# A batched 64x64 matmul on one core: a new order for GpSimd's list, for the casts and turns of VectorE, and for two loads of b

## The chip, the cores and the metric

The kernel runs on one core of a Trainium2 chip. The metric is device time in microseconds (us) from launch to end. A time is compared with runs of the kernel before on the same chip. "PE" is TensorE, "DVE" is VectorE, "ACT" is ScalarE, "POOL" is GpSimd and "SP" is SyncE, as the profile names them.

## The reference

```python
def setup_inputs():
    return {"a": np.random.randn(1024, 64, 64).astype(np.float32),
            "b": np.random.randn(1024, 64, 64).astype(np.float32)}

def reference(a, b):
    return np.matmul(a, b).astype(np.float32)
```

There are 1024 independent products of 64x64 matrices. Each of a, b and the output is 16.78 MB in float32, so 50.33 MB cross between HBM and the core.

## The kernel before

The batch is cut into 16 tiles (t) of 64 matrices, and two tiles make a pair (s = t // 2, eight pairs). A tile is multiplied as block-diagonal matmuls: a's matrices, transposed, stand as small blocks in a 128-row weight tile `at_bd`, and b's matrices stream through. There are two such weight tiles, `bd_tiles[t % 2]`, cleared once.

The steps of a pair s, with their lines:

- `load_a` (L81): three quarters of a's pair are cast to bf16 by GpSimd's DMAs (L76, three per pair), and the last quarter comes as float32 over SyncE (L88). `load_pair` (L112) brings both tiles of b by four casting DMAs on GpSimd's queue (L115). It does so for pairs 1 to 6. The b tiles 0, 1, 14 and 15 come singly as float32 through `load_b` (L104, one DMA of 1 MB, L109). The pools hold three buffers for a and three for b.
- `regroup` (L126): DVE puts the two parts of a side by side in `a_bf` (L130, L133).
- `transpose` (L137): 16 PE transposes per pair into PSUM (L142), 8 for each of j = 0 and j = 1, and four ACT copies to `at_sb` (L145).
- `spread` (L168): four DVE copies per tile put `at_sb` into the diagonal blocks of `at_bd` (L186; for pairs 0 and 1 eight smaller ones, L176). All four copies of one tile read what all four ACT copies of L145 wrote.
- `turn` (L118): a DVE transpose in 32x32 blocks for each half u of b's pair (L124). Every tile of the pair reads both halves.
- `cast` (L191): for b tiles 0, 1, 14 and 15 a copy to bf16 takes the place of the turns.
- `multiply` (L216): 64 matmuls (L247), in two halves of 32, each half into one of two PSUM buffers `o_ps`. `evacuate` (L229) copies each half to `o_sb` by four copies on L235. All of them are on ACT; from tile 10 on DVE takes two of the four copies of the second half, and in the last tile DVE takes half of all.
- `store` (L212): one DMA of 1 MB per tile (L224) on GpSimd's queue, made one tile later than the multiply (`HOLD = 2`). Tile 14 is stored in two pieces and tile 15 in four, on ACT and SyncE.

`tc.manual_schedule()` means that each engine runs its instructions exactly in the order in which the code below L268 writes them; a wait holds everything that is queued behind it on that engine. So the order of the calls in the loop over t is the order on PE, ACT, DVE, and on the queues of GpSimd and SyncE. `multiply(t)` contains its evacuation, so ACT copies of a later call follow the copies of tile t.

Before, the loop works ahead by about two pairs: `spread(t + 1)` stands in front of `multiply(t)`; `regroup(s + 2)` and the first half of `transpose(s + 2)` are made while pair s is multiplied, the second half of the transposes one tile before they are needed, and the turns of the next pair one after each tile. GpSimd's list has the loads of pairs 1 to 4 of b and a up to pair 4 ahead of the first store.

Of the kernel before, what the change touches and what calls it, by code (L numbers as in the profile page):

```python
# [13 lines left out]
def kernel(  # L14
# [14 lines left out]
    nc = tc.nc  # L29
# [8 lines left out]
    HOLD = 2  # L38
    PAIRS = (1, 2, 3, 4, 5, 6)
    ON_DVE = (0, 1)  # L40
    FIRST_B = {1: nc.scalar}

    a_v = a.rearrange("(s g h) (mp v) k -> s h g mp (v k)", h=4, g=32, v=16)
    bp_v = b.rearrange("(s g h) k n -> s h g (k n)", h=4, g=32)
# [36 lines left out]
    def load_a(s, a_sb=None):  # L81
        a_sb = a_sb or cast_load_a(s)
        a_raw = a_pool.tile([128, 16, 64], fp32, name="a_raw")[:].rearrange("p v k -> p (v k)")
        if s in ON_DVE:
            a_raw = a_raw.bitcast(bf16)[:, 0:1024]
            nc.gpsimd.dma_start(out=a_raw, in_=a_v[s, 3], single_packet=True)
        else:
            nc.sync.dma_start(out=a_raw, in_=a_v[s, 3])  # L88
        a_tiles[s] = a_sb, a_raw
# [14 lines left out]
    def load_b(t):  # L104
        b_sb = b_pool.tile([128, 1, 4096], bf16, name="b_sb")[:, 0].bitcast(fp32).rearrange(
            "p (g c) -> p g c", g=16
        )
        queue = FIRST_B.get(t, nc.sync)
        queue.dma_start(out=b_sb, in_=b_v[t])  # L109
        b_tiles[t] = b_sb  # L110

    def load_pair(s):  # L112
        pair = b_pool.tile([128, 1, 4096], bf16, name="b_sb")
        for h in range(4):
            nc.gpsimd.dma_start(out=pair[32 * h : 32 * h + 32, 0], in_=bp_v[s, h])  # L115
        b_tiles[2 * s] = pair
# [20 lines left out]
    def transpose(s, j):  # L137
        a_cols = abf_tiles[s][:].rearrange("p v h k -> p v (h k)").bitcast(fp32)
        for wl in range(2):
            at_ps = t_psum.tile([128, 4, 128], fp32, name="at_ps")  # L140
            for vo in range(4):
                nc.tensor.transpose(  # L142
                    at_ps[:, vo, :], a_cols[:, 4 * vo + 2 * j + wl, :], identity[:]
                )
            nc.scalar.copy(  # L145
                at_tiles[s][:, :, 2 * j + wl, :, :],
                at_ps[:].rearrange("p vo (g mp) -> p g mp vo", mp=4),
            )
# [19 lines left out]
    def spread(t, hs=range(4), copy=nc.vector.tensor_copy):  # L168
        bd = bd_tiles[t % N_BD]
        at_sb = at_tiles[t // 2]  # L170
        for h in hs:
            rows = slice(32 * h, 32 * h + 32)
            if t // 2 in ON_DVE:
                for i in range(2):
                    block = 32 * (2 * (t % 2) + i)
                    copy(  # L176
                        bd[rows, 8 * i : 8 * i + 8, :, h, :, :].rearrange(
                            "p g w mp vo -> p (g w) (mp vo)"
                        ),
                        at_sb[block : block + 32, h].rearrange(  # L180
                            "p g w mp vo -> p (g w) (mp vo)"
                        ),
                    )
            else:
                half = slice(16 * (t % 2), 16 * (t % 2) + 16)
                nc.vector.tensor_copy(  # L186
                    bd[rows, :, :, h, :, :].rearrange("p g w mp vo -> p (g w) (mp vo)"),
                    at_sb[rows, half].rearrange("p g w mp vo -> p (g w) (mp vo)"),
                )
# [26 lines left out]
    def multiply(t):  # L216
        at_bd = bd_tiles[t % N_BD][:].rearrange("p g (j wl) h mp vo -> p j g (wl h mp vo)", j=2)
        at_bd = at_bd.bitcast(bf16).rearrange("p j g (c u) -> p j g c u", u=2)
        b_bf = bbf_tiles[t // 2][:, 16 * (t % 2) : 16 * (t % 2) + 16]
        last = t == n_t - 1  # L220
        o_sb = o_pool.tile([128, 8, 2, 2, 64], fp32, name="o_sb")

        def put(lo, n):
            store_queue(t, lo).dma_start(  # L224
                out=o_v[t, :, lo : lo + n, :],
                in_=o_sb[:, lo : lo + n].rearrange("p gh j wl n -> p (gh j wl n)"),
            )

        def evacuate(o_ps, gh, n, copies):  # L229

            for par in range(2):
                for wl in range(2):
                    src = o_ps[64 * wl : 64 * wl + 64, :, par, :, :]
                    dst = o_sb[64 * par : 64 * par + 64, gh : gh + n, :, wl, :]
                    copies[2 * par + wl](dst, src)  # L235

        for half in range(2):
            if not last:
                o_ps = o_psum.tile([128, 4, 2, 2, 64], fp32, name="o_ps")
            for g8 in range(8):  # L240
                if last and g8 % 4 == 0:
                    o_ps = t_psum.tile([128, 2, 2, 2, 64], fp32, name="at_ps")
                g = 8 * half + g8
                gl = (g8 % 4 if last else g8) // 2
                for j in range(2):
                    for u in range(2):
                        nc.tensor.matmul(  # L247
                            o_ps[:, gl, g % 2, j, :],
                            at_bd[:, j, g, :, u],
                            b_bf[:, g, 64 * u : 64 * u + 64],  # L250
                            start=(u == 0),
                            stop=(u == 1),
                        )
                if last and g8 % 4 == 3:
                    copy = nc.scalar.copy if g8 == 3 else nc.vector.tensor_copy
                    evacuate(o_ps, g // 4 * 2, 2, [copy] * 4)
            if not last:
                copies = [nc.scalar.copy] * 4
                if half and t > 9:
                    copies[2:] = [nc.vector.tensor_copy] * 2  # L260
                evacuate(o_ps, 4 * half, 4, copies)
        if last:
            held[t] = [lambda q=q: put(2 * q, 2) for q in range(4)]
        else:
            whole = t < n_t - 2
            held[t] = [lambda q=q: put(q, 8 if whole else 4) for q in ([0] if whole else [0, 4])]

    with tc.manual_schedule():  # L268
        load_first_a()
        nc.vector.memset(warm[:, 0:1], 0.0)  # L270
        nc.scalar.copy(warm[:, 1:2], warm[:, 0:1])
        load_b(0)
        load_b(1)
        nc.vector.memset(bd_tiles[0][:], 0.0)  # L274
        nc.gpsimd.memset(bd_tiles[1][:], 0.0)  # L275
        load_a(1)
        make_identity(nc, identity)
        load_pair(1)
        load_a(2)
        turn_a(0, 0)  # L280
        spread(0, [0])
        turn_a(0, 1)
        spread(0, [1])
        turn_a(0, 2)
        turn_a(0, 3)
        spread(0, [2], nc.scalar.copy)
        spread(0, [3])
        spread(1)
        cast(0)
        load_pair(2)  # L290
        load_a(3)
        for t in range(n_t):
            s, half = t // 2, t % 2
            if 0 < t < n_t - 1:
                spread(t + 1)
            if t + 1 < n_t:
                cast(t + 1)
            if t == 0:
                load_pair(3)
            if t in (8, 10):  # L300
                load_b(14 + (t - 8) // 2)
            if half == 0 and 1 < s < n_s - 1:
                transpose(s + 1, 1)
            multiply(t)
            if t == 0:
                for h in range(4):
                    turn_a(1, h)
                a_tiles.pop(1)
                load_a(4)
            elif t == 1:  # L310
                turn(1, 0)
                turn(1, 1)
                load_pair(4)
            elif t == 2:
                regroup(2)
                load_a(5)
                transpose(2, 0)
                transpose(2, 1)
                turn(2, 0)
                turn(2, 1)  # L320
                load_pair(5)
            elif t == 3:
                regroup(3)
                load_a(6)
                transpose(3, 0)
            else:
                if s + 1 in PAIRS:
                    turn(s + 1, half)
                    if half and s + 4 in PAIRS:
                        load_pair(s + 4)  # L330
                if half == 0 and s + 2 < n_s:
                    regroup(s + 2)
                    if s + 5 < n_s:
                        load_a(s + 5)
                elif half == 1 and s + 2 < n_s:
                    transpose(s + 2, 0)
            if t >= HOLD - 1:
                store(t - HOLD + 1)
        for t in range(n_t - HOLD + 1, n_t):
            store(t)  # L340

# [29 lines left out]
```

## Time and profile before

| what | value |
|---|---|
| time, median of 3 runs | 135.55 us (134.97 to 136.09) |
| time of the profiled execution | 135.04 us |
| its span, first to last instruction | 133.1 us |
| granted TensorE clock, mean | 0.822 |
| busy: DVE / ACT / PE / POOL | 107.1 / 89.1 / 61.1 / 49.0 us |
| HBM read / written | 33.55 MB / 16.78 MB, 378 GB/s over the span |

The span leaves out 1.94 us that the execution spends around it. Busy times are sums over the span, and their sizes alone do not tell which engine sets the end. In a row of the timeline, "[x <-Y]" means that the engine sat idle for x us before the row and that Y released it.

### The profile page before, as it was taken

How to read it: one execution, taken by the hardware profiler on the slowest of the kernel's cores; microseconds unless marked ns; L12 is line 12 of the kernel's file. 1: busy time of each engine (PE TensorE's matmuls, PEld its weight loads, DVE VectorE, ACT ScalarE, POOL GpSimd, SP SyncE). 2: the span in 40 equal slices, each digit the busy share in tenths (PEclk: the TensorE clock that was granted, in tenths of full speed). 3: DMA queues.
4: the chain of work that ended last, by engine and by line, in shares of the span. 5: the costliest groups of instructions: out<-in, count | busy, mean ns of one | idle time of the engine just before them, and what ended most of it. 6: DMA issues, size and time to landing. Idle time of an engine off the chain costs nothing.

```text
span 133.1 us, 2777 instructions
## 1 busy us (share of the span) xinstructions
PE 61.1 (46%) x1120; PEld 58.3 (44%) x1120; DVE 107.1 (81%) x135; ACT 89.1 (67%) x154; POOL 49.0 (37%) x69
## 2 busy tenths in 40 slices
PE   0000019646490098385763649853028377296000
PEld 0000018636490097385752549853027377285000
DVE  5999849899879994599999999964399948999900
ACT  2364049993999356999999999998206097659300
POOL 8981113432642624270765531345400403042200
PEclk9999999996899757997799985699955955559955
DMA  3999999999999999999999999999999999999992
GB/s 89 393 348 305 313 310 260 245 282 229 197 221 270 209 209 243 222 339 294 227 230 331 259 358 274 337 292 247 387 401 406 397 356 352 329 342 329 317 341 71
DMA packets 13068, 38.45 MB, mean 289 GB/s; under 512 B 1280, under 2 KB 2304, under 8 KB 12288
## 3 DMA queue, kind: packets, MB, share of 16 engines
q0 software_dynamic: 8416, 27.79, 78.2%
q1 hardware_dynamic: 3280, 7.87, 16.8%
q10 hardware_dynamic: 1360, 2.62, 5.3%
q8 instruction: 9, 0.15, 0.4%
q14 instruction: 3, 0.02, 0.1%
HBM read 33.55 MB, written 16.78 MB: 378 GB/s over the span
## 4 chain that ended last, share of the span: by engine, by line
DMA 47%; DVE 17%; ACT 14%; PE 9%; issue 4%; POOL 3%; DVEq 0%; POOLq 0%
DMA a_sb<-in_a_dram 37%; ACT o_sb L235 13%; DMA out_dram<-o_sb 10%; DVE at_bd L186 6%; PE o_ps L247 6%; DVE o_sb L235 5%; PE at_ps L142 3%; DVE b_bf L124 2%; ACT at_sb L145 2%; POOL at_bd L275 1%; DVE a_bf L130 1%; POOL a_sb L76 1%; DVE b_bf L203 1%; DVE a_bf L133 1%; DVE b_bf L208 1%
## 5 line engine op out<-in xcount | busy, mean ns | idle before, releaser
L235 ACT COPY o_sb<-o_ps 64x512 f32<-64x512 f32 x110 | 63.9, 581 | 11.6 <-PE o_ps L247 10.1
L247 PEld LDWEIGHTS <-at_bd 128*128 128x128 bf16 x1024 | 43.5, 113 | 49.5 <-issue 27.4
L247 PE MATMUL o_ps<-b_bf,at_bd 128*128 128x64 bf16 x960 | 43.7, 217 | 46.2 <-ACT b_bf L200 19.5
L186 DVE COPY at_bd<-at_sb 32x1024 f32<-32x1024 f32 x48 | 35.0, 728 | 1.2
L124 DVE STREAM_TRANSPOSE b_bf<-b_sb 128x1024 f32<-128x1024 f32 x12 | 26.4, 2218 | 5.9 <-DMA b_sb<-in_b_dram 5.7
L224 POOL DMA_DIRECT2D out_dram<-o_sb x16 | 16.5, 1032 | 37.4 <-issue 14.7
L142 PE MATMUL at_ps<-identity,a_bf 128*128 128x128 f32 x96 | 16.8, 349 | 14.2 <-DVE a_bf L133 14.2
L115 POOL DMA_DIRECT2D b_sb<-in_b_dram x24 | 14.9, 623 | 18.1 <-DMA b_sb<-in_b_dram 5.9
L142 PEld LDWEIGHTS at_ps<-identity,a_bf 128*128 128x128 f32 x96 | 15.1, 184 | 14.5 <-issue 8.2
L145 ACT COPY at_sb<-at_ps 128x512 f32<-128x512 f32 x24 | 12.9, 596 | 11.0 <-issue 6.2
L76 POOL DMA_DIRECT2D a_sb<-in_a_dram x21 | 13.0, 618 | 19.0 <-DMA a_sb<-in_a_dram 15.9
L176 DVE COPY at_bd<-at_sb 32x512 f32<-32x512 f32 x30 | 12.7, 423 | 0.7
L235 DVE COPY o_sb<-o_ps 64x512 f32<-64x512 f32 x10 | 6.9, 689 | 3.4 <-ACT o_sb L235 3.3
L130 DVE COPY a_bf<-a_sb 128x3072 bf16<-128x3072 bf16 x6 | 5.7, 947 | 3.8 <-DMA a_sb<-in_a_dram 3.8
L155 ACT CAST a_bf<-o_sb 128x1024 bf16<-128x1024 f32 x3 | 3.0, 1044 | 3.5 <-DMA o_sb<-in_a_dram 3.5
L200 ACT CAST b_bf<-b_sb 128x1024 bf16<-128x1024 f32 x1 | 1.0, 1044 | 6.2 <-DMA b_sb<-in_b_dram 6.2
L133 DVE CAST a_bf<-a_raw 128x1024 bf16<-128x1024 f32 x6 | 4.1, 690 | 0.0
L274 DVE MEMSET at_bd<- 128x4096 f32 x1 | 3.5, 3472 | 0.8 <-issue 0.8
L163 DVE STREAM_TRANSPOSE at_sb<-a_bf 128x512 f32<-128x512 f32 x4 | 4.0, 1041 | 0.1
L275 POOL MEMSET at_bd<- 128x4096 f32 x1 | 3.5, 3511 | 0.3 <-POOLq L355 0.3
L235 DVE COPY o_sb<-at_ps 64x256 f32<-64x256 f32 x8 | 3.4, 422 | 0.1
L235 ACT COPY o_sb<-at_ps 64x256 f32<-64x256 f32 x8 | 2.9, 366 | 0.1
(21 smaller groups left out, 17.3 us busy)
## 6 DMA issues: line engine op xcount, KB each, us to landing
out_dram<-o_sb POOLq DMA_DIRECT2D x14, 1024.0 KB, 15.0
b_sb<-in_b_dram POOLq DMA_DIRECT2D x24, 256.0 KB, 12.4
a_sb<-in_a_dram POOLq DMA_DIRECT2D x21, 256.0 KB, 11.8
a_raw<-in_a_dram SPq DMA_DIRECT2D x6, 512.0 KB, 11.9
o_sb<-in_a_dram SPq DMA_DIRECT2D x2, 512.0 KB, 5.4
o_sb<-in_a_dram ACTq DMA_DIRECT2D x2, 512.0 KB, 6.4
out_dram<-o_sb POOLq DMA_DIRECT2D x2, 512.0 KB, 6.9
out_dram<-o_sb ACTq DMA_DIRECT2D x2, 256.0 KB, 6.0
```

The costliest lines, as they stand in the source:

```text
L76: nc.gpsimd.dma_start(out=a_sb[:, h, :, :].rearrange("p v k -> p (v k)"), in_=a_v[s, h], single_packet=True)
L115: nc.gpsimd.dma_start(out=pair[32 * h : 32 * h + 32, 0], in_=bp_v[s, h])
L124: nc.vector.transpose(cols[:, u], rows[:, u])
L130: nc.vector.tensor_copy(a_bf[:, :, 0:3, :], cast_sb[:].rearrange("p h v k -> p v h k"))
L133: nc.vector.tensor_copy(a_bf[:, :, 3, :], raw.rearrange("p (v k) -> p v k", v=16))
L142: nc.tensor.transpose(at_ps[:, vo, :], a_cols[:, 4 * vo + 2 * j + wl, :], identity[:])
L145: nc.scalar.copy(at_tiles[s][:, :, 2 * j + wl, :, :], at_ps[:].rearrange("p vo (g mp) -> p g mp vo", mp=4),)
L176: copy(bd[rows, 8 * i : 8 * i + 8, :, h, :, :].rearrange("p g w mp vo -> p (g w) (mp vo)"), at_sb[block : block + 32, h].rearrange("p g w ...
L186: nc.vector.tensor_copy(bd[rows, :, :, h, :, :].rearrange("p g w mp vo -> p (g w) (mp vo)"), at_sb[rows, half].rearrange("p g w mp vo -> p ...
L224: store_queue(t, lo).dma_start(out=o_v[t, :, lo : lo + n, :], in_=o_sb[:, lo : lo + n].rearrange("p gh j wl n -> p (gh j wl n)"),)
L235: copies[2 * par + wl](dst, src)
L247: nc.tensor.matmul(o_ps[:, gl, g % 2, j, :], at_bd[:, j, g, :, u], b_bf[:, g, 64 * u : 64 * u + 64], start=(u == 0), stop=(u == 1),)
```

## The change

From tile 0 on, the loop calls `multiply(t)` first. `regroup` and both halves of `transpose` work on the next pair (s + 1) and stand behind the multiply of the even tile. Behind the multiply of the odd tile stand the spread of the next even tile, both turns of the next pair, and the spread of the next odd tile. Loads move behind the stores: for t = 2, 4, 6 and 8 GpSimd's list gets, after `store(t - 1)`, the load of b's pair s + 2 and of a's pair s + 3. The b tiles 14 and 15 are asked for by ACT in t = 10, in place of SyncE in t = 8 and 10. `cast(1)` stands ahead of the loop. DVE takes its two copies of the evacuation from tile 12 on, no longer from tile 10.

On GpSimd the list before goes, behind a's pair 3: b pair 3, a pair 4, b pair 4, store 0, a pair 5, b pair 5, store 1, a pair 6, store 2, a pair 7, store 3, b pair 6, stores 4 to 14. After it goes, behind a's pair 3: stores 0 and 1, b pair 3, a pair 4, stores 2 and 3, b pair 4, a pair 5, stores 4 and 5, b pair 5, a pair 6, stores 6 and 7, b pair 6, a pair 7, stores 8 to 14.

```diff
-    FIRST_B = {1: nc.scalar}
+    B_QUEUE = {0: nc.sync, 1: nc.scalar, 14: nc.scalar, 15: nc.scalar}
...
-        queue = FIRST_B.get(t, nc.sync)
-        queue.dma_start(out=b_sb, in_=b_v[t])
+        B_QUEUE[t].dma_start(out=b_sb, in_=b_v[t])
...
-                if half and t > 9:
+                if half and t > 11:
                     copies[2:] = [nc.vector.tensor_copy] * 2
...
         load_a(3)
+        cast(1)
         for t in range(n_t):
             s, half = t // 2, t % 2
-            if 0 < t < n_t - 1:
-                spread(t + 1)
-            if t + 1 < n_t:
-                cast(t + 1)
-            if t == 0:
-                load_pair(3)
-            if t in (8, 10):
-                load_b(14 + (t - 8) // 2)
-            if half == 0 and 1 < s < n_s - 1:
-                transpose(s + 1, 1)
             multiply(t)
             if t == 0:
                 for h in range(4):
                     turn_a(1, h)
                 a_tiles.pop(1)
-                load_a(4)
-            elif t == 1:
-                turn(1, 0)
-                turn(1, 1)
-                load_pair(4)
-            elif t == 2:
-                regroup(2)
-                load_a(5)
-                transpose(2, 0)
-                transpose(2, 1)
-                turn(2, 0)
-                turn(2, 1)
-                load_pair(5)
-            elif t == 3:
-                regroup(3)
-                load_a(6)
-                transpose(3, 0)
-            else:
-                if s + 1 in PAIRS:
-                    turn(s + 1, half)
-                    if half and s + 4 in PAIRS:
-                        load_pair(s + 4)
-                if half == 0 and s + 2 < n_s:
-                    regroup(s + 2)
-                    if s + 5 < n_s:
-                        load_a(s + 5)
-                elif half == 1 and s + 2 < n_s:
-                    transpose(s + 2, 0)
+            elif half == 0 and s + 1 < n_s:
+                regroup(s + 1)
+                transpose(s + 1, 0)
+                transpose(s + 1, 1)
+            elif half and s + 1 in PAIRS:
+                spread(t + 1)
+                turn(s + 1, 0)
+                turn(s + 1, 1)
+                spread(t + 2)
+            elif half and s + 1 < n_s:
+                for later in (t + 1, t + 2):
+                    spread(later)
+                    cast(later)
             if t >= HOLD - 1:
                 store(t - HOLD + 1)
+            if half == 0 and 0 < s < 5:
+                load_pair(s + 2)
+                load_a(s + 3)
+            if t == 10:
+                load_b(14)
+                load_b(15)
```

## The prediction

> **What bounds the kernel now.** I read the page's 40 slices first, then the timelines of ACT, DVE and PE.
>
> ```profile
> DMA  3999999999999999999999999999999999999992
> GB/s 89 393 348 305 313 310 260 245 282 229 197 221 270 209 209 243 222 339 294 227 230 331 259 358 274 337 292 247 387 401 406 397 356 352 329 342 329 317 341 71
> ```
>
> The DMA engines are never free between the first slice and the last. (GB/s counts a casting load by what it writes, half of what it reads, so the 200s of the middle are no slack.) 50.33 MB at the page's 378 GB/s are the whole 133.1 us: the kernel is bound by transfers, and the stores that wait fill the queue while the engines compute ahead. The compute rows show how far ahead. ACT, then DVE:
>
> ```profile
> 32.86 4.74 ACT L235 COPY o_sb<-o_ps 64x512 f32<-64x512 f32 x8 [2.00 <-PE o_ps L247]
> 37.63 2.06 ACT L145 COPY at_sb<-at_ps 128x512 f32<-128x512 f32 x4
> ...
> 51.68 9.50 ACT L235 COPY o_sb<-o_ps 64x512 f32<-64x512 f32 x16 [1.05 <-PE o_ps L247]
> 61.21 2.05 ACT L145 COPY at_sb<-at_ps 128x512 f32<-128x512 f32 x4
> 63.12 9.53 ACT L235 COPY o_sb<-o_ps 64x512 f32<-64x512 f32 x16
> ```
>
> ```profile
> 59.15 2.18 DVE L124 STREAM_TRANSPOSE b_bf<-b_sb 128x1024 f32<-128x1024 f32 x1
> 61.23 2.80 DVE L186 COPY at_bd<-at_sb 32x1024 f32<-32x1024 f32 x4
> 64.06 2.24 DVE L124 STREAM_TRANSPOSE b_bf<-b_sb 128x1024 f32<-128x1024 f32 x1
> 66.53 0.96 DVE L130 COPY a_bf<-a_sb 128x3072 bf16<-128x3072 bf16 x1 [0.23 <-DMA a_sb<-in_a_dram]
> 67.40 0.70 DVE L133 CAST a_bf<-a_raw 128x1024 bf16<-128x1024 f32 x1
> ...
> 110.06 1.39 DVE L235 COPY o_sb<-o_ps 64x512 f32<-64x512 f32 x2 [1.91 <-ACT o_sb L235]
> ```
>
> From 51.7 ACT has no gap: a pair takes 16 copies and 4 at_sb copies, 11.5 us (51.68 to 63.12), while spreads, turns and regroup of another pair run on DVE beside it. The 110.06 row shows that DVE's two copies of a half start only after ACT's two copies of that half. PE:
>
> ```profile
> 31.01 3.50 PE L247 MATMUL o_ps<-b_bf,at_bd 128*128 128x64 bf16 x63 [1.84 <-DVE b_bf L124]
> 36.25 1.94 PE L142 MATMUL at_ps<-identity,a_bf 128*128 128x128 f32 x16 [1.74 <-DVE a_bf L133]
> 38.03 2.03 PE L247 MATMUL o_ps<-b_bf,at_bd 128*128 128x64 bf16 x64
> 46.36 3.65 PE L142 MATMUL at_ps<-identity,a_bf 128*128 128x128 f32 x16 [6.30 <-DVE a_bf L133]
> 49.80 2.77 PE L247 MATMUL o_ps<-b_bf,at_bd 128*128 128x64 bf16 x64
> ...
> 105.25 2.89 PE L247 MATMUL o_ps<-b_bf,at_bd 128*128 128x64 bf16 x63 [2.65 <-DVE b_bf L124]
> ```
>
> Call S(s) the moment when PE has all it needs for the first tile of pair s: S(1) = 31.0, S(2) = 49.8, S(6) = 105.25.
>
> **The turns between the spreads, and the lost lead.** The list up to S(1) is the same in both, so S(1) stays 31.0. Behind it the new order closes a ring. Spread of tile 2s+2 needs all four at_sb copies of pair s+1. On ACT these stand behind the eight copies of tile 2s. DVE, in order, holds both turns behind that spread; and PE needs both turns to start tile 2s+2. Before, these copies were made a pair earlier; now nothing hides them. One ring, by rows:
>
> - S to the end of the at_sb copies. The kernel before has this very sequence once, for tile 2 and pair 2: PE starts at 31.01, the eight copies run 32.86 to 37.60, the four to 37.63 + 2.06 = 39.69. That is 8.7 us.
> - Then four spread copies, 4 x 728 ns = 2.9, and two turns, 2 x 2.21 = 4.4.
>
> Sum 16.0 us per pair, against 11.5 where ACT bounded. The other branch is as long: spread of tile 2s+1 (2.9), regroup (0.95 + 0.69 = 1.6), 16 transposes (mean of six rows 16.8/6 = 2.8), the last at_sb copy (0.6) are 7.9, so a quicker PE saves little. Bounds: with a half multiply at 1.0 (2.03 for 64) in place of 1.8, 15.3; with slow transposes (3.65) and slow multiply, 16.4. I take 16.0, since tile 2 is the same sequence. The ring's spreads of tile 2s+1 and the second evacuation hide in the wait. Five rings: S(6) = 31.0 + 80 = 111.0, against 105.25: +5.75 (bounds 107.5 to 113). It is no more because before loses time twice, 31.0 to 49.8 and 85.25 to 105.25, to transposes that wait for regroup and to b's pair 6.
>
> **The end.** Before, pair 7 was regrouped (97.3) ahead of S(6). Now, from S(6): half of tile 12 on PE 1.45 (mean between 1.0 and 1.8), six ACT copies 3.5, DVE's two copies 1.4: 6.3. Regroup 1.6, transposes 2.8: 10.7. Tile 13, which PE holds behind the transposes, again 1.45 + 3.5 + 1.4: 17.1, and DVE holds spread 14 behind these two copies. Spread 14, 2.9, and cast, 1.2: 21.2. Tile 14 needs 6.3 till DVE has copied its share: 27.5; spread 15 and its cast (2.9 + 1.0) lie beside that. DVE's eight copies of tile 15, 3.5: 31.0. Before, the same stretch is 105.25 to 126.4 (122.91 + 3.48), 21.1. So +9.9 (bounds +7.5 at the fast PE, +12 at the slow).
>
> The last stores of 256 KB took 5.9 us over SP beside a full queue. Now the queue is nearly empty; the shortest landing of an o_sb transfer in the trace is 3.9. I take 2.0 off (bounds 0 to 3).
>
> **GpSimd's list.** Stores 0 and 1 are ready when ACT ends tile 1 at 30.9, and b's pair 3 was issued at 33.0 anyway. Two stores of 1 MB now stand ahead of every pair's loads. The loads have room: store 3 is ready at 44.4 (39.69 and eight copies, 4.7), pair 4 is issued by 49 and turned at S(3) + 11.6 = 74.6, 25 us later; the longest landing in the trace is 17.6 for a b load and 22.1 for o_sb. So 0 on the path. What becomes of the cover if it is gone: each us late is a us on the ring, up to four times. A pair's transfers, 6.29 MB, take 16.6 us at 378 GB/s, so the queue nearly keeps the ring's pace even without its lead of two pairs. POOL's own issues (0.5 to 1.4 each) are on no path.
>
> **b 14 and 15 on ACT.** Two issues of 0.77 (the row of b 1 on ACT), behind the at_sb copies of pair 6 and ahead of tile 11's copies, where ACT waits for PE. Their buffers are free, as pairs 4 and 5 are turned. Issued near S(5) + 8.7 = 103.7, they are wanted at 130; b 1 took 16.5. SP loses two issues that nobody waited for. 0. **Evacuation from tile 12, not 10:** 4 x 0.58 more on ACT, which is in the rings above; DVE loses 4 x 0.69 where it would wait. **cast(1)** follows the same ACT and DVE rows: 0.
>
> Sum on the profiled execution: 135.04 + 5.75 + 9.9 - 2.0 = 148.7. The median is 0.5 above that execution: **149 us**. Bounds by adding the ends: 135.5 + 2.25 + 7.5 - 3 = 142.3 and 135.5 + 7.75 + 12 = 155.3.
>
> The Trainium skill (TensorE: Matmul & The Clock Gate, Part 1) says that PE falls to half its clock after an idle window of about 3.4 us. The trace agrees after 6.30 us of idleness (3.65 for 16 transposes, against 1.94), but also shows 3.65 at 81.17 with no gap, so idle time alone does not tell the clock.
>
> **Rivals.**
> 1. *PE cold in every ring.* In a ring PE ends tile 2s+1 about 11.5 us in and then waits 4.5 us, longer than the 1.84 ahead of the 31.01 row. With every multiply at 3.5 and transposes at 3.65 the rings are 16.4 and the end +12: 135.5 + 7.75 + 12 - 2 = 153. For: 3.50 and 3.65 rows behind waits. Against: 1.94 behind 1.74. The skill's rule, just named, asks for this. 13%.
> 2. *Loads late behind the stores.* The ring becomes the queue's: if the landing of pairs 4 to 6 passes 25 us, each later pair starts some 2 us late, 149 + 4 x 2 = 157. Against: longest b landing 17.6. 7%.
> 3. *Faster: transfers still set the end.* Stores start at 31 and not at 49, so the end has fewer stores left. Store-only slices run at 317 to 342 GB/s, mixed ones at 387 to 406; 50.33 MB at 400 are 126, and some 5 us at the ends and 1.94 around the span make 133. It decides if the ring is below 6.29 MB / 400 = 15.7 and the end stretch no longer than 21 us. The ring is near that bound, but the end stretch speaks against it by 10. 5%.
> 4. *No change:* the ring overlaps better, or a loss in the end meets a gain of the queue. 3%.
>
> **How the numbers follow.** Forecast 72%, at 149. Its bounds 142.3 to 155.3 hold rival 1; rival 2 lies past the top, where I stop at 156. Left out: most of rivals 2 to 4, about 14%, and some of the forecast's tails. One per cent is about what a measurement can tell from no change. Slower by over 1%: 72 + 13 + 7 = 92%; within 3%; faster 5%.
>
> **What would show it.** In the profile after: even tiles' first rows on PE 16 us apart (near 47, 63, 79, 95, 111); DVE idle some 4 us in each ring ahead of a spread, released by ACT's L145; ACT with gaps in place of 11.5 us of unbroken copies; DMA slices below 9 in the second half; store 0 issued near 32; the last DVE copy near 142. It would be wrong if DVE does not wait ahead of the spreads, if turns wait for DMA (rival 2), or if slices of 9 run to the end.

## The result, and the profile after

The changed kernel takes 153.06 us (median of 4 runs, 151.63 to 154.0) against 135.26 us for the kernel before: 1.128 times as long, 95% interval 1.116 to 1.140. The profiled execution took 152.69 us, with a span of 150.9 us, against 135.04 and 133.1. The profiled executions are 17.65 us apart, the medians 17.8. One of the four runs, at 154.0 us, was a slow one, and the ratio leaves it out.

The page's slices of the changed kernel, as shown for the kernel before:

```profile
PEclk9999999969595699755995569789955557755855
DMA  3999999999999999999999999999999380043484
GB/s 113 400 322 305 310 267 249 274 226 198 298 410 269 194 280 406 298 201 270 413 300 203 270 397 240 200 290 355 314 379 286 136 278 4 0 174 104 136 283 144
```

The transfers are no longer busy to the end. Up to slice 30 (counted from 0, about 117 us) they are as busy as before. In the last nine slices (some 34 us) they are mostly free, and in slices 33 and 34 they move almost nothing. The stores are not late; there is nothing to store yet. So the end is set by the engines.

The timeline of DVE over one ring, and behind it the end stretch from tile 12 on:

```profile
96.22 2.79 DVE L185 COPY at_bd<-at_sb 32x1024 f32<-32x1024 f32 x4
99.05 0.96 DVE L129 COPY a_bf<-a_sb 128x3072 bf16<-128x3072 bf16 x1
99.92 0.69 DVE L132 CAST a_bf<-a_raw 128x1024 bf16<-128x1024 f32 x1
105.06 2.83 DVE L185 COPY at_bd<-at_sb 32x1024 f32<-32x1024 f32 x4 [4.45 <-ACT at_sb L144]
107.92 4.22 DVE L123 STREAM_TRANSPOSE b_bf<-b_sb 128x1024 f32<-128x1024 f32 x2
...
117.63 1.39 DVE L234 COPY o_sb<-o_ps 64x512 f32<-64x512 f32 x2 [2.53 <-ACT o_sb L234]
119.05 0.96 DVE L129 COPY a_bf<-a_sb 128x3072 bf16<-128x3072 bf16 x1
119.93 1.05 DVE L132 CAST a_bf<-a_raw 128x1024 bf16<-128x1024 f32 x1
130.04 1.39 DVE L234 COPY o_sb<-o_ps 64x512 f32<-64x512 f32 x2 [9.06 <-ACT o_sb L234]
131.46 3.09 DVE L185 COPY at_bd<-at_sb 32x1024 f32<-32x1024 f32 x4
```

After spread and regroup DVE stands still for 4.45 us until ACT has written `at_sb`; only then come the next spread and both turns. At the end it stands still for 9.06 us between regroup and the two copies of tile 13, with spread 14 behind them. The same ring on ACT (ACTq rows are issues of its DMA queue):

```profile
98.21 4.74 ACT L234 COPY o_sb<-o_ps 64x512 f32<-64x512 f32 x8 [3.59 <-PE o_ps L246]
...
102.97 1.07 ACT L144 COPY at_sb<-at_ps 128x512 f32<-128x512 f32 x2
...
103.93 0.60 ACT L144 COPY at_sb<-at_ps 128x512 f32<-128x512 f32 x1
104.07 3.15 ACTq L108 DMA_DIRECT2D b_sb<-in_b_dram  x1
104.41 0.62 ACT L144 COPY at_sb<-at_ps 128x512 f32<-128x512 f32 x1
107.31 4.74 ACT L234 COPY o_sb<-o_ps 64x512 f32<-64x512 f32 x8 [2.29 <-issue]
```

And PE, with the starts of tiles 10 and 12 and the end stretch:

```profile
96.36 3.38 PE L246 MATMUL o_ps<-b_bf,at_bd 128*128 128x64 bf16 x63 [1.83 <-DVE b_bf L123]
...
112.20 3.52 PE L246 MATMUL o_ps<-b_bf,at_bd 128*128 128x64 bf16 x63 [1.80 <-DVE b_bf L123]
121.04 3.68 PE L141 MATMUL at_ps<-identity,a_bf 128*128 128x128 f32 x16 [5.32 <-DVE a_bf L132]
124.51 3.06 PE L246 MATMUL o_ps<-b_bf,at_bd 128*128 128x64 bf16 x64
135.87 3.59 PE L246 MATMUL o_ps<-b_bf,at_bd 128*128 128x64 bf16 x64 [8.30 <-DVE b_bf L202]
```

The ring can be read off these rows: PE starts at 96.36, ACT's eight copies run 98.21 to 102.95, the four at_sb copies to 105.03, the spread to 107.89, the turns to 112.14, and PE starts the next pair at 112.20. No step of it overlaps another: 1.85 + 4.74 + 2.08 + 2.86 + 4.25 + 0.06 = 15.84 us.

### The profile page after: what moved, and what is told of

Read it like the earlier page. It is cut to its first block, busy times and chain, and to the rows that moved or that the text cites. A ratio compares the mean times of both kernels' runs of the same rounds, so it can differ in the third digit from the quotient of the medians.

```text
span 150.9 us, 2765 instructions
## 1 busy us (share of the span) xinstructions
PE 66.4 (44%) x1120; PEld 63.6 (42%) x1120; DVE 104.4 (69%) x131; ACT 91.6 (61%) x160; POOL 47.1 (31%) x69
## 5 line engine op out<-in xcount | busy, mean ns | idle before, releaser
L234 ACT COPY o_sb<-o_ps 64x512 f32<-64x512 f32 x114 | 66.1, 580 | 33.6 <-PE o_ps L246 29.9
L246 PEld LDWEIGHTS <-at_bd 128*128 128x128 bf16 x1024 | 47.9, 119 | 64.8 <-DVE b_bf L123 23.9
L246 PE MATMUL o_ps<-b_bf,at_bd 128*128 128x64 bf16 x960 | 47.3, 225 | 63.0 <-DVE b_bf L123 34.1
L185 DVE COPY at_bd<-at_sb 32x1024 f32<-32x1024 f32 x48 | 34.5, 718 | 22.0 <-ACT at_sb L144 20.9
L223 POOL DMA_DIRECT2D out_dram<-o_sb x16 | 15.9, 992 | 53.3 <-ACT o_sb L234 17.4
L123 DVE STREAM_TRANSPOSE b_bf<-b_sb 128x1024 f32<-128x1024 f32 x12 | 25.4, 2164 | 1.2 <-DMA b_sb<-in_b_dram 1.0
L141 PE MATMUL at_ps<-identity,a_bf 128*128 128x128 f32 x96 | 17.9, 364 | 12.4 <-DVE a_bf L132 12.4
L141 PEld LDWEIGHTS at_ps<-identity,a_bf 128*128 128x128 f32 x96 | 15.9, 192 | 13.3 <-DVE a_bf L132 10.8
L114 POOL DMA_DIRECT2D b_sb<-in_b_dram x24 | 13.4, 561 | 13.3 <-DMA b_sb<-in_b_dram 7.3
L234 DVE COPY o_sb<-o_ps 64x512 f32<-64x512 f32 x6 | 4.1, 689 | 13.7 <-ACT o_sb L234 11.6
L129 DVE COPY a_bf<-a_sb 128x3072 bf16<-128x3072 bf16 x6 | 6.3, 1044 | 0.2
```

Of the source, the lines that this page charges most:

```text
L123: nc.vector.transpose(cols[:, u], rows[:, u])
L129: nc.vector.tensor_copy(a_bf[:, :, 0:3, :], cast_sb[:].rearrange("p h v k -> p v h k"))
L141: nc.tensor.transpose(at_ps[:, vo, :], a_cols[:, 4 * vo + 2 * j + wl, :], identity[:])
L185: nc.vector.tensor_copy(bd[rows, :, :, h, :, :].rearrange("p g w mp vo -> p (g w) (mp vo)"), at_sb[rows, half].rearrange("p g w mp vo -> p ...
L223: store_queue(t, lo).dma_start(out=o_v[t, :, lo : lo + n, :], in_=o_sb[:, lo : lo + n].rearrange("p gh j wl n -> p (gh j wl n)"),)
L246: nc.tensor.matmul(o_ps[:, gl, g % 2, j, :], at_bd[:, j, g, :, u], b_bf[:, g, 64 * u : 64 * u + 64], start=(u == 0), stop=(u == 1),)
```

## Experiments

Times are medians. Ratios are to runs of the kernel before on the same chip, with the 95% interval.

**The list alone.** The engines' order of the kernel before, with the changed lists of loads and stores, and b 14 and 15 asked for by ACT.

```diff
 (in the kernel before)
-            if t == 0:
-                load_pair(3)
...
-                load_a(4)
... (all later load_pair and load_a calls, and load_b in t = 8 and 10, taken out)
             if t >= HOLD - 1:
                 store(t - HOLD + 1)
+            if half == 0 and 0 < s < 5:
+                load_pair(s + 2)
+                load_a(s + 3)
+            if t == 10:
+                load_b(14)
+                load_b(15)
```

> GpSimd's new list and b 14 and 15 on ACT, but the engines' order of the kernel before (regroup two pairs ahead, one turn behind each tile). Ring theory (the wait of DVE for the at_sb copies costs the time): no ring, so ACT again runs pairs back to back and transfers set the end: 133 to 140 us, DVE's idle time ahead of the spreads under 5 us in all. Queue theory (loads late behind the stores): most of the loss stays, 148 us or more.

Measured: 140.24 us, 1.038 (1.034 to 1.043). That is 12.8 us below the changed kernel and 5.2 above the kernel before, just past the top of what the ring theory gave. PE's start of tile 12 tells where:

```profile
111.04 3.48 PE L246 MATMUL o_ps<-b_bf,at_bd 128*128 128x64 bf16 x63 [3.01 <-DVE b_bf L123]
```

Tile 12 starts at 111.04 us, hardly ahead of the changed kernel (112.20) and 5.8 us behind the kernel before (105.25). From there to the end of the span are 27.0 us, against 38.7 and 27.9. So of the 12.8 us only 1.2 came back ahead of tile 12 and 11.7 in the end stretch (by the spans): up to tile 12 the new list by itself costs nearly as much as the ring does. The waits of DVE for loads (sum in us, times, longest):

```profile
DVE b_bf L123 <- DMA b_sb<-in_b_dram: 8.9, 3, 5.6
DVE a_bf L129 <- DMA a_sb<-in_a_dram: 3.8, 3, 1.6
```

No row of DVE waits for at_sb any more; it waits 12.7 us for loads, most of which stand behind stores. The same waits are 5.7 and 3.8 in the kernel before. Their sum is no price: it differs by 3.2 us where 5.2 are lost, and a later variant (e9) waits 15.2 us and is as fast as the kernel before. The transfers show the loss better. Up to tile 12 they are as busy in all three kernels (DMA share 1.04 in the changed one, 1.05 here, 1.06 before). From tile 12 on the share is 0.48 over 39 us, 0.69 over 27 and 0.91 over 28. Worked out from these shares, an estimate of the time in which nothing moves there is 20, 8 and 3 us: 18 and 6 more than before, about what the two kernels lose.

**The order alone.** The changed order of the engines, with the loads put as early as their buffers allow.

```diff
                 a_tiles.pop(1)
+                load_pair(3)
+                load_a(4)
...
                 transpose(s + 1, 1)
+                if s + 4 < n_s:
+                    load_a(s + 4)
...
                 turn(s + 1, 1)
+                if s + 4 in PAIRS:
+                    load_pair(s + 4)
                 spread(t + 2)
...
-            if half == 0 and 0 < s < 5:
-                load_pair(s + 2)
-                load_a(s + 3)
```

> The changed engines' order, but the loads of a and b as early in GpSimd's list as their buffers allow, ahead of the stores as in the kernel before. Ring theory: the starts of the even tiles stay 16 us apart and the time stays at 150 to 155 us. Queue theory: loads come early, so 140 us or less.

Measured: 152.91 us, 1.134 (1.128 to 1.139), the same as the changed kernel. The even tiles start between 31.48 and 112.22 us, 16.1 apart on average. Its waits have this row of DVE:

```profile
DVE at_bd L185 <- ACT at_sb L144: 21.8, 5, 4.5
```

Five waits of about 4.4 us, one in each ring, whatever the list. So the order of the engines alone makes the whole loss, and the list adds nothing on top of it. The two parts do not add up (5.2 and 17.8 alone, 17.8 together): loads that would be late are in time for a slower ring. In the changed kernel b's pairs 3 to 6 land 5.9 to 10.2 us ahead of their turns.

**A longer ring.** Each at_sb copy on ACT made twice.

```diff
+            for _ in range(2):
                 nc.scalar.copy(
                     at_tiles[s][:, :, 2 * j + wl, :, :],
```

> The changed kernel with each of the four at_sb copies of a pair made twice on ACT (0.5 to 0.6 us each, 2.1 to 2.4 a pair), for pairs 2 to 7. Ring theory: these copies stand in the ring, so the rings of pairs 2 to 6 grow by 2 us or more each, and the time by 10 to 13 us: 162 to 167. Queue theory (ACT has 40% of its time free): within 2 us of the changed kernel.

Measured: 164.39 us, 1.212 (1.204 to 1.219), 11.3 above the changed kernel. On PE the even tiles now start at 31.41, 50.25, 68.56, 86.86, 105.16 and 123.46: rings of 18.3 after the first. The five rings together take 123.46 - 31.41 = 92.05 us against 112.20 - 31.44 = 80.76, so 11.3 more, or 2.26 each. ACT is busy for only 61% of the changed kernel's span, and still what is added at this place of the ring comes back in full. The copies of pair 7 were doubled too, but the end stretch did not grow (162.2 - 123.46 = 38.7): there ACT had waited for PE between these copies and behind them.

**The end repaired.** Regroup of pair 7 behind spread 13, and DVE's copies from tile 14 on.

```diff
-                if half and t > 11:
+                if half and t > 13:
...
             elif half == 0 and s + 1 < n_s:
-                regroup(s + 1)
+                if s + 1 < n_s - 1:
+                    regroup(s + 1)
...
                 spread(t + 2)
+                if t == 11:
+                    regroup(7)
```

> The changed kernel with regroup of pair 7 put behind spread 13, ahead of tile 12's evacuation, and DVE's copies from tile 14 on in place of 12. Ring theory with the end stretch as counted: transposes of pair 7 start some 4.6 us behind the start of tile 12 in place of 8.8, spread 14 no longer stands behind tile 13's copies, and tile 14 starts some 13 to 15 us behind tile 12 in place of 23.7: 143 to 146 us. Rival (the end is set by stores or by b 14 and 15): 151 or more.

Measured: 142.09 us, 1.053 (1.048 to 1.057), 11.0 below the changed kernel and a little better than expected. PE from tile 12 on:

```profile
112.71 3.79 PE L246 MATMUL o_ps<-b_bf,at_bd 128*128 128x64 bf16 x63 [0.24 <-DVE b_bf L123]
117.01 2.65 PE L141 MATMUL at_ps<-identity,a_bf 128*128 128x128 f32 x16 [0.51 <-DVE a_bf L132]
119.49 2.03 PE L246 MATMUL o_ps<-b_bf,at_bd 128*128 128x64 bf16 x64
125.61 3.42 PE L246 MATMUL o_ps<-b_bf,at_bd 128*128 128x64 bf16 x64 [4.08 <-DVE b_bf L202]
```

Tile 12 starts where it did (112.71), tile 14 starts 12.9 us behind it in place of 23.7. From tile 12 to the end of the span are 27.4 us (140.1 - 112.71); the kernel before takes 27.9 (133.1 - 105.25). So the loss of the changed kernel is about 11 us in the end stretch and, for the rest, the stage of the rings: tile 12 at 112.20 against 105.25, 6.95 us. The two edits were made together, and no run tells their shares. With the end repaired and the ring kept, this kernel is only 1.85 us slower than the list alone, which has no ring: by these two runs, taking the ring away wins little as long as the new list stays.

**b 14 and 15 on SP**, in the changed kernel and in the list alone.

```diff
-    B_QUEUE = {0: nc.sync, 1: nc.scalar, 14: nc.scalar, 15: nc.scalar}
+    B_QUEUE = {0: nc.sync, 1: nc.scalar, 14: nc.sync, 15: nc.sync}
```

> The changed kernel, b tiles 14 and 15 asked for by SP in place of ACT, at the same place of the list. Ring theory: the 3.15 us that ACT spent on issuing b 15 were covered by the wait for pair 6, so the same time within 1% (151.5 to 154.5). Rival (ACT's issue delays tile 11 and with it the end): 2 us less, 151 or below.

Measured: 153.10 us, 1.134 (1.129 to 1.139), the same.

> e1_list_alone with b 14 and 15 asked for by SP in place of ACT. Theory that its 5 us over the kernel before come from loads that land late (DVE waited 12.6 us for them): the same time within 1%, 139 to 141.5. Rival (ACT, held for 5.21 us by the issue of b 15, delays tile 11 and DVE's copies): 137 or less.

Measured: 144.31 us, 1.065 (1.055 to 1.075). Both expectations fell: it is 4.1 us slower than with ACT asking. SP's timeline and DVE's waits in this kernel:

```profile
81.34 16.67 SPq L108 DMA_DIRECT2D b_sb<-in_b_dram  x2
```

```profile
DVE b_bf L123 <- DMA b_sb<-in_b_dram: 8.0, 3, 5.1
DVE a_bf L129 <- DMA a_sb<-in_a_dram: 7.8, 4, 3.4
```

SP, with nothing else to do, asks for b 14 at 81.3 as soon as a buffer is free; ACT, in its place of the list, asks at 96.88. The float32 load of 1 MB, wanted only by tile 14, then shares the engines with pair 6 and a's last pairs, which are wanted first: DVE's waits for a double (3.8 to 7.8 us), and tile 12 starts at 115.35 in place of 111.04. In e1 ACT's queue was held by the issue of b 15 for 5.21 us, but DVE worked without a gap from 99.32 us to the start of tile 12, so that hold did not delay it. In the changed kernel the early load costs nothing (e3), where SP asks at 80.5 us: its loads have time to spare.

**PE kept busy.** 24 more transposes behind each odd tile from 3 to 11, whose results nobody reads.

```diff
             elif half and s + 1 in PAIRS:
+                if s > 0:
+                    keep_busy(s + 1, 24)   # 24 PE transposes into an at_ps tile
                 spread(t + 1)
```

> The changed kernel with 24 more PE transposes (never read) behind each odd tile from tile 3 to 11, in the wait for the turns. Clock theory (the 4 us above the forecast are slow matmuls behind PE's waits): the first tile of each ring takes 2.0 to 2.8 us in place of 3.5, rings of 15.4 to 15.8 us, 149 to 151 us. Rival (the clock does not follow PE's idle time): the first tiles still take 3.4 or more and the time stays at 152 to 155.

Measured: 153.37 us, 1.129 (1.120 to 1.138), no gain. PE in the fourth ring, and its busy time and granted clock from 33 to 112 us:

```profile
92.38 2.82 PE L153 MATMUL at_ps<-identity,a_bf 128*128 128x128 f32 x24
95.97 0.20 PE L252 MATMUL o_ps<-b_bf,at_bd 128*128 128x64 bf16 x1 [0.77 <-DVE b_bf L123]
98.01 3.45 PE L252 MATMUL o_ps<-b_bf,at_bd 128*128 128x64 bf16 x63 [1.84 <-DVE b_bf L123]
```

```profile
33.00:112.00 79.00, 57.92 (x828) 0.74 1.03 288
```

The transposes themselves ran fast (2.82 us for 24), yet the multiply behind them, after two short waits, took 3.45 us, and the granted clock was 0.74; the changed kernel has 41.37 us of PE work and 0.76 in the same stretch. Two rings had quicker first tiles (2.80 and 2.41), but their transposes then took 3.68 and the rings did not shrink. Filling PE's waits with transposes does not buy the quick clock; whether transposes count for the clock as matmuls do, and what matmuls in these waits would do, no run shows. What sets the granted clock here stays open.

**Towards a better kernel.** Three variants of the kernel before, and one that combines two of them.

```diff
 e7:  -if half and t > 9:                  +if half and t > 13:
 e9:  list as in the change, but load_pair(3) and load_a(4) in t = 0, then behind the
      store of t = 2, 4, 6: load_pair(s + 3) and load_a(s + 4); b 14, 15 on SP; t > 13
 e10: b 14 and 15 asked for by ACT behind the stores of t = 9 and t = 11
 e11: e9 with the loads of b 14 and 15 as in e10
```

> The kernel before, with DVE's copies of the evacuation from tile 14 on in place of tile 10. The chain of DVE from 95 to 126 us loses 8 copies of 0.69. If the compute chain sets the end of the kernel before, 131 to 134 us; if the transfers do (slices of 9 to the end), within 1% of before.

> The order of the kernel before, GpSimd's list alternating as in the change but with the loads of one more pair ahead of the stores, b 14 and 15 on SP at tiles 8 and 10, DVE's copies from tile 14 on. If late loads cost list alone its 5 us, the lead of one pair gives them back: 132 to 137 us. If the alternation itself costs (reads and writes mixed), 139 or more.

> The kernel before, with b 14 and 15 asked for by ACT behind tiles 9 and 11 in place of SP as soon as a buffer is free (73.6 and 85.3 us). Theory from e1 against e8 (an early float32 load of b 14 takes the engines from pair 6 and a's pair 7, which are wanted first): pair 6 lands some 2 to 3 us ahead of 95.2 and tile 12 starts earlier; as transfers stay busy to the end the time falls by 0 to 3 us, 132 to 135. Rival (the queue sets the end whatever the order): within 1% of before.

> e9_one_pair_earlier with b 14 and 15 asked for by ACT behind tiles 9 and 11. Same theory: 131 to 134 us, and pair 6 and a's pair 7 land earlier than in e9. Rival: within 1% of e9.

Measured: e7 135.44 us, 1.004 (1.001 to 1.008). This does not tell transfers from engines: the copies went to ACT, DVE now waits 3.95 us for ACT near the end, and its last copy ends at 126.6 us, as before (126.4). e9 135.50 us, 1.001 (0.997 to 1.005): alternating loads and stores need not cost anything. That it was the lead of one pair is not shown alone, since e9 differs from the list alone also in DVE's copies and in the engine that asks for b 14 and 15. Its tile 12 starts at 109.44 us, 1.6 ahead of e1 and 4.2 behind the kernel before; its end stretch is 2.6 us shorter than that of e1 (24.4 against 27.0).

e10 134.16 us, 0.994 (0.991 to 0.998), and e11 134.29 us, 0.993 (0.989 to 0.997), just past its range. In e10 pair 6 lands at 92.2 us against 95.15, as expected; tile 12 starts 2.8 us and DVE's last copy ends 2.1 us earlier than before, but the span is only 0.9 us shorter, with the transfers busy almost to its end. This, and not e7, is what speaks for transfers that set the end of the kernel before. Both intervals lie below 1, by about half a per cent, which is less than the one per cent that I set as the bound of what can be told from no change.

## Why the prediction was right

**The ring.** Right as described. Forecast: 16.0 us a ring, S(1) = 31.0, S(6) = 111.0. Measured: 31.44, 48.00, 63.82, 80.23, 96.36, 112.20, a mean of 16.15. The term was +5.75 and came to +6.95. DVE's five waits ahead of a spread sum to 20.9 us, 4.2 each, as forecast. Of the 1.2 us that were missing 0.44 stand ahead of S(1) and 0.76 in the five rings. In the first, third and fourth ring the last at_sb copy also waited 0.2 to 0.3 us for PE's transposes: the "other branch" of the prediction, which it had called as long. The order alone (e2) and the longer ring (e6) show that the ring paces the pairs. No run makes the ring shorter; a pair's 6.29 MB in 16.15 us are 389 GB/s, so the transfers were close behind it, and without the ring (e1) pairs 2 to 6 came 15.3 us apart.

**The end.** The steps were right and this term was too small: +9.9 forecast, 34.08 - 21.1 = +13.0 measured, outside its own bounds of +7.5 and +12. The whole stayed in the range because the ring and the stores were inside theirs. From the start of tile 12 (112.20) to DVE's last copy (146.28):

| step | forecast | measured |
|---|---|---|
| tile 12, to the end of DVE's copies | 6.3 | 6.8 |
| regroup, transposes of pair 7 | 4.4 | 5.5 |
| tile 13, to the end of DVE's copies | 6.4 | 6.9 |
| spread 14, cast, to the start of tile 14 | 4.1 | 4.4 |
| tile 14, to the end of DVE's copies | 6.3 | 6.9 |
| tile 15, DVE's eight copies | 3.5 | 3.5 |

The step that failed is "half of tile 12 on PE 1.45 (mean between 1.0 and 1.8)", used three times, and with it the mean of 2.8 for the transposes: ACT's first copies started 1.85, 1.95 and 1.92 us behind PE's starts, and the transposes took 3.68, so that tile 13 started 3.5 us behind their start. In a chain where PE starts afresh each time, the slow rows of the kernel before were the ones to take, not their mean with quick ones. That is 1.4 + 0.7 of the 3.1 us that were missing; regroup (2.0 in place of 1.6) gave 0.4, and the rest is spread over the other steps.

**Last stores.** Forecast 6.7 - 2.0 = 4.7 from DVE's last copy to the end of the span, measured 150.9 - 146.28 = 4.6; the 256 KB stores landed in 3.1 to 4.6 us.

**GpSimd's list, b on ACT.** Priced at 0, and 0 in this kernel: e2 and e3 equal it. The cover that the prediction named was real: without the ring the list costs 5.2 us (e1). It was thinner than reckoned: pair 4 was issued at 51.6 to 55.1 us, not by 49, and landed 6.5 us ahead of its turn at 75.94. The issue of b 15 was priced at 0.77 and took 3.15 us; ACT's tile 11 began 2.3 us later for it, but ended (112.05) before tile 12 had anything to copy.

**Rivals.** Rival 1 named 153 us, which is what was measured, and in the sizes it was nearer than the forecast: slow multiplies came at the start of every ring (3.38 to 3.52), and the end stretch went past its slow bound. Its transposes were not slow throughout (1.97 in two of five rings), its rings were 16.15 and not 16.4, and its cause, the long wait, is not borne out. In e5 the 63 matmuls took 3.45 us after waits of 0.77 and 1.84 us, with 24 quick transposes ahead of them. The kernel before shows the same without transposes in between:

```profile
77.11 1.09 PE L247 MATMUL o_ps<-b_bf,at_bd 128*128 128x64 bf16 x32 [1.51 <-ACT o_sb L235]
79.50 1.86 PE L247 MATMUL o_ps<-b_bf,at_bd 128*128 128x64 bf16 x32 [1.29 <-ACT o_sb L235]
```

The second 32 matmuls took 1.86 us against 1.09, and no wait of PE since 49.80 had been longer than 2.01 us. The Trainium skill (TensorE: Matmul & The Clock Gate, Part 1) has the slow clock come after about 3.4 us of idleness; here it also came without such a wait, and on that the measurement decides.

Rival 2 (loads late) does not show in this kernel: the only wait of the turns for b, 1.0 us, stands ahead of pair 1, whose loads no store precedes. It comes out only where the ring is gone. Rival 3 needed transfers busy to the end; the slices show them free.

**The signs.** The even tiles' starts, DVE's waits for ACT and the gaps on ACT came as named, and store 0 was issued at 33.6 us. Two signs did not come: slices of 9 run on to slice 30, well into the second half, and DVE's last copy ended at 146.3 us and not near 142.

## What to carry to other kernels

When every engine runs its list in order, follow one result once around all the lists: a step that is moved from "two pairs ahead" to "just ahead" can close a ring through three engines, none of which is more than 70% busy, and the ring's length is then the pace. Before a ring is taken out, ask what waits right behind it: here the list alone delays tile 12 by 5.8 us and the ring by 6.95, and the end stretch, where nothing was left to overlap, was the larger loss. Two losses that lie in parallel do not add, so reverting one part of a change can show nothing (e3) although the same edit costs 4 us elsewhere (e8). Ask for a load neither later nor much earlier than its turn: one that is wanted last and asked for first delays those that are wanted first.

## What the hardware showed that was not expected

- A second 1 MB load in runs of 512 B, asked for by ACT 1.2 us behind the first, held ACT's queue for 3.15 us in the changed kernel, 5.21 in the list alone, and 1.18 (e6) to 4.41 (e2) in others; asked for 14 us later (e10) its issue took 0.70 us.
- The granted clock did not follow PE's busy time: 40% more of it in the same 79 us, most of it transposes, left the clock at 0.74 against 0.76.
